# A two-block fp32 network on one core: products on disjoint tiles of the array made neighbours in TensorE's order

## The chip, the cores and the metric

The kernel runs on one core of a Trainium2 chip. The metric is the device time of one execution in microseconds (us), the median of several. TensorE (PE) multiplies; loading its stationary operand is shown as an engine of its own (PEld). VectorE (DVE), ScalarE (ACT) and GpSimd (POOL) do the rest, and SyncE (SP) issues the transfers.

## What is computed

The reference takes 256 tokens of width 1024 through two stacks of two layers each, all in fp32. Cut to what the change touches:

```python
def first_block(x, ...):           # layer 0: recurrence beside differential attention; layer 1: gated MLP
    y_r = rwkv7_mix(...)           # 8 heads of 64; in the kernel: chunks, with a triangular solve
    y_d = diff_attention(...)      # softmax(q1 k1) - lam * softmax(q2 k2), heads of 64, causal
    x = layer_norm(ALPHA * x + concat(y_r, y_d) @ w_out); x = layer_norm(ALPHA * x + conv_ffn(x))
    ...

def second_block(x, c, ctx, ...):  # 256 tokens and 256 of a context, two layers
    m = silu(c) @ w_mod + b_mod    # modulation: 1024 -> 6144, for c and for c_ctx
    h = rms_norm(x) * (1 + scale) + shift
    o_f = fourier_mix(...); o_a = window_attention(...); o_h = hgrn_bidir(...)
    x = x + gate * (sum(sigmoid(g_i) * (o_i @ w_i)) @ w_out)
    x = x + gate2 * (square(relu(h2 @ w1)) @ w2)
```

## The kernel before, in words

**Large products.** Weights stream in 512 KB tiles `wraw` (four buffers, L222), issued by SP. Each is split into a high part `whi` (ScalarE) and a low part `wlo` (VectorE), and every product is three matmuls: high by high, high by low, low by high, with 128 rows and 128 columns of the array in use.

**Small products.** Several products use only a part of the array and are in plain fp32, for which the trace has two matmuls for each call of `mm`. Five kinds of them stand in places that belong together, since they use parts that do not overlap:

- modulation (L1096, the product at L1108): for each of 8 feature chunks and 3 column quads of two layers, four products of 512 columns go to four tiles of 32 array columns, from two `wraw` tiles into one PSUM bank `sf`;
- recurrence pairs (`wkv`, L809): for each of 4 (token tile, head group) pairs and two head pairs, the products of `bt` and `kt` with `ar`, the even head on array rows 0 to 63 and the odd on rows 64 to 127, each half into a PSUM bank of its own; VectorE then multiplies each bank by a mask into `M`;
- scores, in differential attention (`scores`, L1021) and in window attention (`attention`, L1478): `qT` by `kT`, again one product on each half of the array's rows, into two banks; masks are added by further matmuls, then follow maximum, exponential, reciprocal;
- values of window attention (L1509): probabilities `PT` of two heads by `va`, one head on array columns 0 to 63, one on 64 to 127, over four key blocks (two for the context's queries and so on), into one bank;
- sums of squares (`ss_chunk`, L1200): after each fourth column chunk, the squares `sq` (four buffers for each half of the tokens, L1194) times ones, on four tiles of 32 array columns.

Banks: `ss` has two buffers (L226), `st` two, `mm` three, `sf` one. `ss` serves the recurrence, all scores and the state-space branch.

**What sets the order.** The program is written as a sequence of calls, in which generators interleave stages by hand: `fill` (L1087) puts one modulation step between steps of others, `merge` steps (L1688) go between attention steps. At build time a scheduler then sets each engine's order from the tiles' dependences and from priorities that follow the program's order. On the chip each engine takes its instructions in that order, and semaphores stand where another engine's result is needed. No product of a run is tied to the next one: what else is ready may be placed between them.

Of the kernel before, what the change touches and what calls it, by code (L numbers as in the profile page):

```python
# [18 lines left out]
S = 256  # L19
KC = D // 128  # L20
# [8 lines left out]
# columns of per-feature parameters: feature = chunk * 128 + partition  # L29
# [184 lines left out]
class Kern:  # L214
# [60 lines left out]
    def mm(self, out, lhsT, rhs, start=True, stop=True, **k):  # L275
        self.pe.matmul(out, lhsT, rhs, start=start, stop=stop, **k)  # L276
# [47 lines left out]
    def w_stat(self, out, hi, lo, xh, xl, nk, start=True, stop=True, k0=0):  # L324
        """out[cols, tok] += w^T x, weights stationary; hi, lo [128, nk * 128]."""
        for k in range(nk):
            wh, wl = hi[:, k * 128:(k + 1) * 128], lo[:, k * 128:(k + 1) * 128]
            a, b = xh[:, k0 + k], xl[:, k0 + k]
            self.mm(out, wh, a, start=start and k == 0, stop=False)
            self.mm(out, wh, b, start=False, stop=False)  # L330
            self.mm(out, wl, a, start=False, stop=stop and k == nk - 1)

    def w_stat_steps(self, out, hi, lo, xh, xl, nk):
        """w_stat in steps of two feature chunks."""
        for k in range(0, nk, 2):
            self.w_stat(out, hi[:, k * 128:], lo[:, k * 128:], xh, xl, 2, k == 0, k == nk - 2, k)
            yield

    def w_stat_k(self, items, xh, xl, nk=KC):
        """Several column chunks at once, feature chunk outermost: each chunk of x is used as it arrives.  # L340
        items: (out, hi, lo, first of its bank)."""
        for k in range(nk):
            for out, hi, lo, first in items:
                wh, wl = hi[:, k * 128:(k + 1) * 128], lo[:, k * 128:(k + 1) * 128]
                a, b = xh[:, k], xl[:, k]
                self.mm(out, wh, a, start=first and k == 0, stop=False, skip_group_check=True)
                self.mm(out, wh, b, start=False, stop=False, skip_group_check=True)
                self.mm(out, wl, a, start=False, stop=k == nk - 1, skip_group_check=True)

    def w_mov(self, outs, hi, lo, xh, xl, nk, ncol, toks, first, last, k0=0):  # L350
        """outs[i][tok, cols] += x^T w for token tile toks[i], weights moving."""
        for i, t in enumerate(toks):
            for k in range(nk):
                wh, wl = hi[:, k * ncol:(k + 1) * ncol], lo[:, k * ncol:(k + 1) * ncol]
                a, b = xh[:, k0 + k, t * 128:(t + 1) * 128], xl[:, k0 + k, t * 128:(t + 1) * 128]
                self.mm(outs[i], a, wh, start=first and i % 2 == 0 and k == 0, stop=False, skip_group_check=True)
                self.mm(outs[i], a, wl, start=False, stop=False, skip_group_check=True)
                self.mm(outs[i], b, wh, start=False, stop=last and k == nk - 1, skip_group_check=True)

    def nat_gemm(self, w, cb, xh, xl, toks, nh=2):  # L360
        """Column block cb (256 wide) of x @ w in token-major banks, two token tiles to a bank."""
        banks = [self.pmm() for _ in range(len(toks) // 2)]
        outs = [banks[i // 2][:, (i % 2) * 256:(i % 2) * 256 + 256] for i in range(len(toks))]
        for h in range(nh):
            hi, lo = self.wload(w[cb * nh + h])
            self.w_mov(outs, hi, lo, xh, xl, 4, 256, toks, h == 0, h == nh - 1, k0=4 * h)
        return [b.rearrange("p (t c) -> p t c", t=2) for b in banks]

# [42 lines left out]
    def norm_rows(self, i):  # L411
        """Gain and bias of the i-th norm, on every partition."""
        rows = self.lr.tile([128, 2, D], F32, name="lrow")
        self.nc.sync.dma_start(rows.rearrange("p a c -> p (a c)"),
                                 self.A["lnrows"][i:i + 1].partition_broadcast(128))
        return rows

    def nat_out(self, w, yh, yl, z, early=1):
        """z = ALPHA * z + y @ w; for the first column blocks the half of y that is ready first goes ahead of the other."""
# [20 lines left out]
    def last_block(self, z, yh, yl, tiles, scale=1.0, banks=None, first=True, last=True):  # L440
        """Last column block of z = scale * z + y @ w, a bank for each token tile."""
# [9 lines left out]
    def layer_norm(self, z, nm, l, rows, final=None):  # L451
        """Normalise token-major z. Gives the split transposed activations, and the norm in z, or, in the end, the
        residual of the second block."""
# [176 lines left out]
    def shift_mix(self, pool, bank, chunks, tag):  # L630
        """xs = p + mu * (previous token's p - p), features on partitions."""
# [163 lines left out]
    def wkv(self, es, side, ar, bt, kt, vn, bn, kn, gn, pend, bon, wmask, wlev, row):  # L795
# [7 lines left out]
        for t, g in groups:  # L803
            for j in (2 * g, 2 * g + 1):
                banks = [self.pss(), self.pss()]
                tk = slice(t * 128, t * 128 + 128)
                for i, w in enumerate((bt, kt)):
                    for ps, e in zip(banks, (slice(0, 64), slice(64, 128))):
                        self.mm(ps[:, i * 256:i * 256 + 256], w[e, j, tk], ar[e, j, t])  # L809
# [149 lines left out]
    def to_feat(self, y, c0, t):  # L959
        """Token-major y [128, 512] of token tile t into split chunks c0.. of the transposed activations."""  # L960
# [39 lines left out]
    def diff_attn(self, es, qT, kT, vd, row):  # L1000
# [14 lines left out]
        def scores(t, h):  # L1015
# [3 lines left out]
            for c in range(2):  # L1019
                e = slice(64 * c, 64 * c + 64)  # L1020
                self.mm(pv[c][:, :nk], qT[e, h, t * 128:(t + 1) * 128], kT[e, h, :nk], start=True, stop=False)  # L1021
# [65 lines left out]
    def fill(self, n):  # L1087
        """Emit n steps of the work that waits in self.fillers."""
# [7 lines left out]
    def modulation(self, l, quads):  # L1096
        """Columns quad * 2048.. of silu(cond) @ w_mod + b_mod, both conditions, features on partitions.
        Four 512-column blocks go through four 32-column tiles of the array."""
        for qd in quads:
            ps = self.psf()  # L1100
            for k in range(KC):
# [5 lines left out]
                for j in (2, 3, 0, 1):  # L1107
                    self.mm(ps[32 * j:32 * j + 32], self.cs[:, k],  # L1108
                            raws[j // 2][:, (j % 2) * 512:(j % 2) * 512 + 512],
                            start=k == 0, stop=k == KC - 1, skip_group_check=True)  # L1110
# [14 lines left out]
    def second_setup(self):  # L1125
        """Constants of the second block, the residual (x | ctx, features on partitions), and the context's first norm."""
# [32 lines left out]
    def lower_bounds(self, cp):  # L1159
        """Forget-gate bounds of both layers, [128, dir * 4 + head]; f = th * cf + df, k = th * ck + dk."""  # L1160
# [31 lines left out]
    def ss_chunk(self, ap, k, s):  # L1192
# [4 lines left out]
        if k % 4 == 3:  # L1197
            for k, sl, sq in [q for q in self.ssq if q[1] == sl]:
                j = k % 4
                self.mm(self.ssb[32 * j:32 * j + 32, sl], self.ones[:, 0:32], sq,  # L1200
                        start=j not in self.ss_open, stop=k >= 4, skip_group_check=True)
                self.ss_open.add(j)
            self.ssq = [q for q in self.ssq if q[1] != sl]

    def norm_half(self, ap, l, n, s):
        """Modulated norm of one half of the residual into the split hh, hl."""
# [30 lines left out]
    def head_gemm(self, banks, tiles, T, x_first=True):  # L1237
        """First products after a norm: feature chunk outermost, one half after the other."""
# [6 lines left out]
    def head_load(self, w):  # L1245
        """The first three column chunks that follow a norm, two of them into buffers of their own."""
# [4 lines left out]
    def res_chunks(self, l, m, T, w, xh, xl, gate, norm=None, head=None, out=None):  # L1251
        """X += gate * (w^T x), then the norm given by norm = (layer, index); gives the weights that head loads."""
# [145 lines left out]
    def attention(self, l, T, es, br):  # L1398
# [68 lines left out]
        for s in range(T // S):  # L1467
# [3 lines left out]
            for j in range(4):  # L1471
                PT = [ab.tile([128, 4, S], F32, name=f"PT{e}", bufs=1) for e in range(2)]
                for qt in range(2):
                    banks = [self.pss(), self.pss()]
                    for e, ps in enumerate(banks):
                        r = slice(64 * e, 64 * e + 64)
                        q = qT[r, j, s * S + qt * 128:s * S + qt * 128 + 128]
                        self.mm(ps[:, :nk], q, kT[r, k0:], start=True, stop=s == 1)  # L1478
# [26 lines left out]
                po = self.pst()  # L1505
                for k in kc:
                    for e in range(2):
                        r = slice(64 * e, 64 * e + 64)
                        self.mm(po[r, 0:S], va[:, k, r], PT[e][:, k], start=k == kc[0], stop=k == 3)  # L1509
# [33 lines left out]
    def hgrn(self, l, T, es, br, vn, side):  # L1543
# [6 lines left out]
        def parity(tl, s, o, n, B):  # L1550
            """Positions o.. of stream s: blocks of B, the even ones from tl[:, s, 0], the odd ones from tl[:, s, 1]."""
# [7 lines left out]
        def project(h, o):  # L1559
            """Gates, keys, queries and output gate of head h into o, in small steps."""  # L1560
# [127 lines left out]
    def merge(self, l, n, T, br, acc, tgp, mx=None):  # L1688
        """acc += 2 * sigmoid(gate_n) * (branch_n @ w_branch_n), in small steps; the last branch
        splits the sum into mx."""  # L1690
# [23 lines left out]
    def store(self, op, k0, n):  # L1714
        """Feature chunks k0.. of the finished residual, token-major, to the output."""
# [48 lines left out]
```

## Time and profile before

| | |
|---|---|
| median of 3 runs | 2304.64 us (2303.82 to 2312.74) |
| profiled execution, span from first to last instruction | 2304.2 us |
| TensorE busy | 2230.4 us, 97% |
| VectorE, ScalarE, GpSimd busy | 1354.0, 931.6, 294.7 us |
| transfers | 310.06 MB, 135 GB/s on average |

The profile gives no other time for the profiled execution than its span, which lies 0.4 us below the median of the runs. A group's busy time is the union of its instructions: what runs side by side is counted once, and the mean duration beside it counts each by itself. A line of the timeline gives the start, the time from the first start to the last end, and how many like instructions follow each other; an idle time in brackets comes with what ended it.

### The profile page before, as it was taken

What the parts mean: (1) busy time and instruction counts of PE and PEld (TensorE: products, weight loads), DVE (VectorE), ACT (ScalarE), POOL (GpSimd) and SP (SyncE); (2) the same over time, 40 slices, a digit from 0 to 9 for tenths busy, and PEclk for the clock granted to TensorE, in tenths of its full rate; (3) what the DMA queues carried; (4) which work ended last, traced back from release to release, by engine and by line L of the source; (5) the groups of instructions that cost most, each with busy time, mean ns of one, the idle gap of its engine ahead of it and who ended that gap; (6) DMA issues with size and microseconds to landing.
All of it is one profiled execution on the core that took longest, in us unless ns stands there. A gap on an engine that the chain in (4) does not pass through costs nothing. (4 is left out here: it accounts for less than half of the span.)

```text
span 2304.2 us, 37682 instructions
## 1 busy us (share of the span) xinstructions
PE 2230.4 (97%) x15048; PEld 1936.7 (84%) x15048; DVE 1354.0 (59%) x2361; ACT 931.6 (40%) x1589; POOL 294.7 (13%) x382
## 2 busy tenths in 40 slices
PE   8999899989999999999999999999999999999999
PEld 7867799978899988657778888888889878888999
DVE  6523777674867734665566446444345566766665
ACT  5322454442445433442333334233244443345443
POOL 1153200022100002001222000000000205420000
PEclk9999999997999999999999999999999999999999
DMA  7456666573665522123442242333333233245663
GB/s 237 135 170 212 201 206 185 171 242 95 222 188 168 174 74 83 51 85 105 150 136 74 87 119 73 92 101 92 101 111 93 74 95 94 90 133 165 183 183 128
DMA packets 90640, 310.06 MB, mean 135 GB/s; under 512 B 10257, under 2 KB 12433, under 8 KB 89826
## 3 DMA queue, kind: packets, MB, share of 16 engines
q1 hardware_dynamic: 90242, 307.30, 43.1%
q8 instruction: 118, 1.93, 0.3%
q14 instruction: 56, 0.46, 0.1%
q0 software_dynamic: 224, 0.36, 0.0%
HBM read 306.58 MB, written 1.05 MB: 134 GB/s over the span
## 5 line engine op out<-in xcount | busy, mean ns | idle before, releaser
L242 DVE TENSOR_TENSOR wlo<-wraw,whi 128x1024 fp32r<-128x1024 f32 x462 | 558.0, 1211 | 391.4 <-ACT whi L321 390.4
L321 ACT CAST whi<-wraw 128x1024 fp32r<-128x1024 f32 x494 | 492.8, 1001 | 726.2 <-PE mm L276 624.4
L276 PE MATMUL mm<-hh,whi 128*128 128x256 f32 (+1 forms) x1200 | 412.9, 346 | 4.3 <-ACT hh L254 2.4
L276 PE MATMUL mm<-hh,wlo 128*128 128x256 f32 (+1 forms) x1200 | 406.3, 339 | 0.0
L276 PE MATMUL mm<-hl,whi 128*128 128x256 f32 (+1 forms) x1200 | 405.4, 338 | 0.0
L276 PE MATMUL mm<-xh,whi 128*128 128x256 f32 x880 | 252.7, 288 | 8.2 <-ACT xh L321 7.3
L276 PE MATMUL mm<-xl,whi 128*128 128x256 f32 x880 | 253.8, 288 | 3.8 <-DVE xl L242 3.7
L276 PEld LDWEIGHTS mm<-hh,whi 128*128 128x128 f32 x1200 | 227.2, 190 | 32.4 <-issue 7.9
L276 PEld LDWEIGHTS mm<-hh,wlo 128*128 128x128 f32 x1200 | 227.7, 190 | 28.8 <-issue 3.6
L276 PE MATMUL mm<-xh,wlo 128*128 128x256 f32 x880 | 251.9, 286 | 0.0
L276 PEld LDWEIGHTS mm<-hl,whi 128*128 128x128 f32 x1200 | 228.0, 190 | 25.4 <-issue 3.1
L276 PE MATMUL mm<-whi,hh 128*128 128x256 f32 x736 | 205.9, 280 | 3.2 <-ACT vn L1326 2.4
L276 PE MATMUL mm<-whi,hl 128*128 128x256 f32 x736 | 205.6, 279 | 0.0
L276 PE MATMUL mm<-wlo,hh 128*128 128x256 f32 x736 | 205.5, 279 | 0.0
L276 PEld LDWEIGHTS mm<-xh,whi 128*128 128x128 f32 x880 | 171.5, 195 | 10.8 <-ACT xh L321 7.6
L276 PEld LDWEIGHTS mm<-xl,whi 128*128 128x128 f32 x880 | 171.8, 195 | 8.7 <-DVE xl L242 6.8
L276 PE MATMUL mm<-ul,whi 128*128 128x256 f32 (+1 forms) x536 | 176.7, 330 | 0.1
L276 PE MATMUL mm<-uh,wlo 128*128 128x256 f32 (+1 forms) x536 | 176.3, 329 | 0.0
L276 PE MATMUL mm<-uh,whi 128*128 128x256 f32 (+1 forms) x536 | 176.2, 330 | 0.0
L276 PEld LDWEIGHTS mm<-xh,wlo 128*128 128x128 f32 x880 | 171.8, 195 | 0.0
L276 PEld LDWEIGHTS mm<-whi,hh 128*128 128x128 f32 x736 | 140.0, 190 | 4.2 <-ACT vn L1326 2.8
L276 PEld LDWEIGHTS mm<-whi,hl 128*128 128x128 f32 x736 | 138.2, 188 | 0.8 <-issue 0.8
(411 smaller groups left out, 3959.8 us busy)
## 6 DMA issues: line engine op xcount, KB each, us to landing
wraw<-in_w_ff SPq DMA_DIRECT2D x128, 512.0 KB, 3.7
wraw<-in_w_mod SPq DMA_DIRECT2D x96, 512.0 KB, 4.2
wraw<-in_w_up SPq DMA_DIRECT2D x88, 512.0 KB, 3.7
wraw<-in_w_gate SPq DMA_DIRECT2D x48, 512.0 KB, 3.6
wraw<-in_w_dn SPq DMA_DIRECT2D x32, 512.0 KB, 3.6
wraw<-in_w_br SPq DMA_DIRECT2D x48, 256.0 KB, 2.6
wraw<-in_w_h SPq DMA_DIRECT2D x24, 512.0 KB, 3.7
wraw<-in_w_out SPq DMA_DIRECT2D x16, 512.0 KB, 3.8
```

Of the source, the lines that this page charges most:

```text
L242: (eng or self.dve).tensor_tensor(out, a, b, ALU.subtract)
L276: self.pe.matmul(out, lhsT, rhs, start=start, stop=stop, **k)
L321: self.act.copy(hi, src)
```

## The change

A helper `mm_run` issues a list of products. The first is issued as before. Each later one is issued with raised priority and with an edge, without synchronisation, from the one before it. `mm` now returns its instruction. The five kinds of products go through the helper, and in four of them the order within the run is turned round: the second half (or the last chunk, or `kt` before `bt`) comes first. Modulation keeps its order. The rest of the diff removes comments and docstrings.

```diff
     def mm(self, out, lhsT, rhs, start=True, stop=True, **k):
-        self.pe.matmul(out, lhsT, rhs, start=start, stop=stop, **k)
+        return self.pe.matmul(out, lhsT, rhs, start=start, stop=stop, **k)
+
+    def mm_run(self, calls):
+        first = self.mm(*calls[0][:3], **calls[0][3])
+        for out, lhsT, rhs, k in calls[1:]:
+            with self.tc.high_priority():
+                nxt = self.mm(out, lhsT, rhs, **k)
+            self.tc.add_manual_dep(
+                nxt.ins, first.ins.name,
+                mybir.DependencyInfo(mybir.DependencyClass.NoSync, mybir.DependencyReason.DATA), reason="mm_run")
+            first = nxt
...
-                for i, w in enumerate((bt, kt)):
-                    for ps, e in zip(banks, (slice(0, 64), slice(64, 128))):
-                        self.mm(ps[:, i * 256:i * 256 + 256], w[e, j, tk], ar[e, j, t])
+                halves = list(zip(banks, (slice(0, 64), slice(64, 128))))[::-1]
+                self.mm_run([(ps[:, i * 256:i * 256 + 256], w[e, j, tk], ar[e, j, t], {})
+                             for i, w in ((1, kt), (0, bt)) for ps, e in halves])
...
-            for c in range(2):
+            calls = []
+            for c in (1, 0):
                 e = slice(64 * c, 64 * c + 64)
-                self.mm(pv[c][:, :nk], qT[e, h, t * 128:(t + 1) * 128], kT[e, h, :nk], start=True, stop=False)
+                calls.append((pv[c][:, :nk], qT[e, h, t * 128:(t + 1) * 128], kT[e, h, :nk],
+                              dict(start=True, stop=False)))
+            self.mm_run(calls)
...
-                for j in (2, 3, 0, 1):
-                    self.mm(ps[32 * j:32 * j + 32], self.cs[:, k],
-                            raws[j // 2][:, (j % 2) * 512:(j % 2) * 512 + 512],
-                            start=k == 0, stop=k == KC - 1, skip_group_check=True)
+                self.mm_run([
+                    (ps[32 * j:32 * j + 32], self.cs[:, k], raws[j // 2][:, (j % 2) * 512:(j % 2) * 512 + 512],
+                     dict(start=k == 0, stop=k == KC - 1, skip_group_check=True)) for j in (2, 3, 0, 1)])
...
-                self.mm(self.ssb[32 * j:32 * j + 32, sl], self.ones[:, 0:32], sq,
-                        start=j not in self.ss_open, stop=k >= 4, skip_group_check=True)
+                calls.append((self.ssb[32 * j:32 * j + 32, sl], self.ones[:, 0:32], sq,
+                              dict(start=j not in self.ss_open, stop=k >= 4, skip_group_check=True)))
                 self.ss_open.add(j)
+            self.mm_run(calls[-1:] + calls[:-1])
...
-                    for e, ps in enumerate(banks):
+                    calls = []
+                    for e in (1, 0):
...
-                        self.mm(ps[:, :nk], q, kT[r, k0:], start=True, stop=s == 1)
+                        calls.append((banks[e][:, :nk], q, kT[r, k0:], dict(start=True, stop=s == 1)))
+                    self.mm_run(calls)
...
+                calls = []
                 for k in kc:
-                    for e in range(2):
+                    for e in (1, 0):
                         r = slice(64 * e, 64 * e + 64)
-                        self.mm(po[r, 0:S], va[:, k, r], PT[e][:, k], start=k == kc[0], stop=k == 3)
+                        calls.append((po[r, 0:S], va[:, k, r], PT[e][:, k], dict(start=k == kc[0], stop=k == 3)))
+                self.mm_run(calls)
```

## Rows read from the trace of the kernel before

**Rows 1.** The page: span, and busy time of the engines.

```profile
span 2304.2 us, 37682 instructions
PE 2230.4 (97%) x15048; PEld 1936.7 (84%) x15048; DVE 1354.0 (59%) x2361; ACT 931.6 (40%) x1589; POOL 294.7 (13%) x382
```

**Rows 2.** Who waited for whom: us in total, times, longest us.

```profile
ACT whi L321 <- PE mm L276: 624.4, 320, 4.9
```

**Rows 3.** Groups by shape: count | busy us, mean ns | idle before; fourth line: 200 to 246 us.

```profile
L276 PE MATMUL sf<-wraw,cs 128*32 128x512 f32 x384 | 68.5, 621 | 2.0 <-DMA wraw<-in_w_mod 2.0
L276 PE MATMUL ss<-kT,qT 64*128 64x512 f32 x64 | 31.1, 641 | 0.0
L276 PE MATMUL ss<-kT,qT 64*128 64x256 f32 x48 | 13.3, 428 | 0.0
L276 PE MATMUL ss<-kT,qT 64*128 64x128 f32 x16 | 3.9, 322 | 0.0
L276 PE MATMUL st<-PT,va 128*64 128x256 f32 x160 | 27.6, 390 | 0.0
L276 PE MATMUL st<-sq,ones 128*32 128x256 f32 x112 | 20.2, 391 | 0.8 <-ACT sq L254 0.8
```

**Rows 4.** Timeline of TensorE in the triangular solve: start us, us, what, count.

```profile
145.75 1.04 PE L276 MATMUL sf<-wraw,cs 128*32 128x512 f32 x2
150.28 1.04 PE L276 MATMUL sf<-wraw,cs 128*32 128x512 f32 x2
...
172.52 1.07 PE L276 MATMUL sf<-wraw,cs 128*32 128x512 f32 x8
175.94 1.06 PE L276 MATMUL sf<-wraw,cs 128*32 128x512 f32 x8
```

**Rows 5.** Timeline of TensorE at scores, of differential and of window attention.

```profile
225.76 0.70 PE L276 MATMUL ss<-kT,qT 64*128 64x256 f32 x4
915.47 1.12 PE L276 MATMUL ss<-kT,qT 64*128 64x512 f32 x2
940.26 1.63 PE L276 MATMUL ss<-kT,qT 64*128 64x512 f32 x4
949.00 1.91 PE L276 MATMUL ss<-kT,qT 64*128 64x512 f32 x4
979.51 1.13 PE L276 MATMUL ss<-kT,qT 64*128 64x512 f32 x4
```

**Rows 6.** Timeline of TensorE at the values.

```profile
944.18 1.94 PE L276 MATMUL st<-PT,va 128*64 128x256 f32 x14
1035.52 1.08 PE L276 MATMUL st<-PT,va 128*64 128x256 f32 x6
```

**Rows 7.** Timeline of TensorE at the sums of squares.

```profile
718.12 0.64 PE L276 MATMUL st<-sq,ones 128*32 128x256 f32 x8
```

**Rows 8.** Groups by shape: maximum and exponential of the scores.

```profile
L254 ACT ACTIVATE E<-ss,m 128x512 f32<-128x512 f32 x32 | 22.0, 687 | 21.8 <-DVE m L248 21.2 <-DVE m L239 0.5
L1486 DVE TENSOR_REDUCE m<-ss 128x1 f32<-128x512 f32 x32 | 21.6, 685 | 3.0 <-PE ss L276 2.7
```

**Rows 9.** Busy time in stretches: PE, PEld, DVE, ACT, POOL, clock, DMA share, GB/s.

```profile
100.00:125.00 25.00, 22.11 (x148) 16.34 (x147) 10.31 (x16) 1.76 (x3) 13.63 (x27) 1.00 0.20 66
175.00:200.00 25.00, 24.92 (x210) 18.85 (x208) 5.04 (x9) 7.86 (x15) 16.34 (x27) 1.00 0.75 253
```

**Rows 10.** Timeline of TensorE and VectorE at the pairs of the recurrence.

```profile
107.09 0.70 PE L276 MATMUL ss<-ar,bt 64*128 64x256 f32 x4
108.25 1.29 DVE L236 TENSOR_TENSOR M<-ss,wmask 128x512 f32<-128x512 f32 x2 [9.50 <-PE ss L276]
116.60 0.70 PE L276 MATMUL ss<-ar,bt 64*128 64x256 f32 x2 [0.77 <-DVE M L236]
118.51 0.70 PE L276 MATMUL ss<-ar,bt 64*128 64x256 f32 x2 [0.19 <-DVE M L236]
123.50 1.29 DVE L236 TENSOR_TENSOR M<-ss,wmask 128x512 f32<-128x512 f32 x2 [0.62 <-PE ss L276]
```

More of the change, by code (lines that the diff above doesn't have):

```diff
@@ L1505, in attention @@
                 po = self.pst()
+                calls = []
                 for k in kc:
-                    for e in range(2):
+                    for e in (1, 0):
                         r = slice(64 * e, 64 * e + 64)
-                        self.mm(po[r, 0:S], va[:, k, r], PT[e][:, k], start=k == kc[0], stop=k == 3)
+                        calls.append((po[r, 0:S], va[:, k, r], PT[e][:, k], dict(start=k == kc[0], stop=k == 3)))
+                self.mm_run(calls)
                 sl = slice(s * S, s * S + S)
```

## The prediction, made before the result was known

> **What bounds the kernel now.** I read the page first. TensorE is busy 97% of the 2304.2 us span, VectorE 59%, ScalarE 40% [rows 1]. Then I asked who waits for whom: the longest wait of the kernel is ScalarE's, 624.4 us of waiting for matmuls to give back a weight buffer before it splits the next tile [rows 2]. So the weights are ahead, TensorE is the bound nearly everywhere, and what matters is how long it is held by each product, not how late its operands are.
>
> Next, the groups of TensorE instructions by shape [rows 3]. Their busy time is a union: matmuls that run beside each other count once. An fp32 product stands in the trace as two matmuls (192 modulation products, 384 matmuls). For the five kinds that the change touches I compare this union with the length of one complete run, taken from the timeline. Modulation: eight matmuls (four products on four column tiles) take 1.07 us, but two matmuls of one product alone take 1.04 us [rows 4]. A product that stands alone therefore costs as much as four. Scores: a pair on two row tiles takes 1.13 us, one alone 1.12 us; at 256 columns a pair takes 0.70 us [rows 5]. The saving is the number of pieces into which runs are broken.
>
> That a piece really holds TensorE is seen in the triangular solve, where one kernel shows both. With one of four modulation products cut off from its run, the cycle from one such stray to the next is 150.28 - 145.75 = 4.53 us; with runs whole it is 175.94 - 172.52 = 3.42 us [rows 4]. The 1.11 us between them is one piece of 1.04 us and a little for going in and out of the column tiles. In the whole-run stretch the DMA engines were 75% busy at 253 GB/s [rows 9], and TensorE 24.92 of 25 us: the faster pace was fed.
>
> **The change part by part.** *The helper.* Returning the instruction, the order edge (without synchronisation) and the priority add no instruction: TensorE should keep 15048 matmuls [rows 1]. Cost nothing on chip; if some edges became semaphore waits, it would show as time in which the engine waits for nothing visible, a rival below.
>
> *Modulation, L1108.* 48 runs of four. Now 68.5 us; whole 48 x 1.07 = 51.4; gain 17.1 us [rows 3, 4]. The order of the products does not change, so their transfers are waited for as before. Buffers of `wraw` come free earlier, which lets SP issue the next load earlier.
>
> *Scores, L1021 and L1478.* Each fp32 call gives two matmuls: 64, 48 and 16 matmuls are 16, 12 and 4 pairs. At 512 columns 31.1 - 16 x 1.13 = 13.0 us; at 256, 13.3 - 12 x 0.70 = 4.9; at 128, I let the 3.9 us halve, 1.9, as if none of the four pairs were whole now; the other end is 0, if all were [rows 3, 5]. Sum 19.8 us. The upper half now goes first, so a run waits until both `ss` banks are free, where half of it could go when the first was. Queued behind it on TensorE is whatever was placed next; waiting for it are the maximum (0.685 us) and the exponential (0.687 us) of each half [rows 8]. Cover: a bank pair's round is 1.1 us for the run and 2.1 for two maxima and one exponential; with as much as the run again for masks and gaps, an estimate, some 4.3 us. Runs of scores stand 8.7 us apart (940.26 to 949.00) [rows 5, 8], so there are 4 us of slack with merge products between. If that cover goes, the whole 19.8 is at stake.
>
> *Values, L1509.* 12 runs: eight of eight products (four key blocks, two heads; four in each layer) and four of four (the context's queries, first layer). The first product goes alone now, when the first half's probabilities are there, and the rest follows later, as 14 or 6 matmuls [rows 6]. 8 x 1.95 + 4 x 1.08 = 19.9 against 27.6: gain 7.7 us; 1.95 is the 14 matmuls at 1.94, to which two more go beside others. The run starts with the half that VectorE copies last.
>
> *Sums of squares, L1200.* 56 products are 14 runs: 20.2 - 14 x 0.64 = 11.2 us [rows 3, 7]. Three squares of a run are held until the fourth is there. They have four buffers; the next square is one column chunk later and the run itself is 0.64 us, so this costs nothing; without that gap it would be up to 0.64 us for ScalarE, 14 times.
>
> *Pairs of the recurrence, L809.* Here the cover is missing. In the steady part a unit takes 118.51 - 116.60 = 1.91 us because one bank is filled while VectorE reads the other, and TensorE waits on M [rows 10]. With the upper half first, a run starts after both reads: 1.16 us from a whole run's start to the first read (107.09 to 108.25), and 1.29 for two reads: 2.45 us. Eight units end at 107.09 + 8 x 2.45 = 126.7 instead of 123.50 + 1.29 = 124.8: **1.9 us lost**. The other end: of the 1.91 us TensorE is idle 0.19 and held 1.72, where a whole run holds it 1.16; if modulation runs move into the gap, 8 x 0.56 = 4.5 us are won [rows 10]. I take the loss, since the stretch shows TensorE idle for M already.
>
> The Trainium skill (TensorEngine Tiling (Array Packing), section PSUM Bottleneck) says that tiling speeds up TensorE and not the emptying of PSUM, which may then bound. Rows 10 agree for the recurrence; elsewhere the slack above speaks against it. By it the scores' part would be left out of the sum, which is the first rival.
>
> *Sum.* 17.1 + 19.8 + 7.7 + 11.2 = 55.8 us of TensorE time. Not all becomes time: the emptiest of the stretches with such runs shows TensorE busy 22.11 of 25 us (88%), another 24.92 [rows 9]. As work leaves, stretches come nearer to the first; I take 88%: 49.3. Less 1.9: 47.4 us. The profiled execution has a span of 2304.2 us, 0.4 below the median of the runs, 2304.64; I count from the median: **2257 us**. With 100% and the 4.5 us it would be 2304.6 - 60.3 = 2244.
>
> **Rivals.** *Bank hand-over takes the scores' gain.* Runs wait for the second bank, and 19.8 us come back as waits on ScalarE's exponential. For: two banks only, and the recurrence shows it. Against: the 4 us of slack. (55.8 - 19.8) x 0.88 - 1.9 = 29.8: 2275 us. The rule quoted above from the Trainium skill (TensorEngine Tiling (Array Packing), PSUM Bottleneck) would end here.
>
> *Half is lost to new waits.* The order on TensorE is fixed ahead, and moving a hundred runs shifts what stands between; chains now hidden (transposes of E, of Q) come out. For: TensorE sits idle for 2.9 of 25 us where its operands come out of short chains [rows 9]. Against: the stretch with the whole modulation runs stayed full. 27.9 - 1.9 = 26.0: 2279 us.
>
> *It does not do what it says.* If the scheduler lets other ready work between a product and its follower, runs stay as they are: 2304.6 us, no change.
>
> *Slower: the head of the queue.* A run begins with the operand that comes last, and TensorE issues in order, so if that operand is later on the chip than where the run was placed, everything behind waits. The place is the start of the 48 + 32 + 12 + 14 + 8 = 114 runs; the price is bounded by the worst adjacent pair now, 1.91 us where 1.13 would do [rows 5], 0.78 us. At that price everywhere 89 us against 55.8: 2338 us. It decides from 0.49 us a run on. Against: other pairs waited far less (1.63 us, a 0.50 us wait, and none at 979.51).
>
> **How the numbers follow.** Forecast 0.64, bank hand-over 0.13, half lost 0.11, no effect 0.06, slower 0.06. The range reaches from just below all gains with none lost (2242) past the two rivals of the same sign (2283) and leaves out the last two. About 0.5% (11.5 us) is what a measurement can tell from no change: forecast and the first two rivals are faster by more, 0.88; 0.06 same; 0.06 slower.
>
> **What would show it.** Right: modulation's busy time near 51 us in 48 stretches of eight matmuls; scores near 18, 8 and 2; values near 20; squares near 9; a solve cycle of 3.4 us throughout; the recurrence's pairs about 2.45 us apart. Wrong: the same unions as now (no effect); unions fallen, but TensorE's idle time up, before scores on ScalarE (hand-over) or before transposes and weights elsewhere (half lost); waits at the head of runs near 0.5 us each (slower).

## The result, and the profile of the changed kernel

The changed kernel takes **2280.2 us** (median of 4 runs, 2275.4 to 2283.8) where the kernel before took 2304.3 in the same series: a ratio of **0.9885 [0.9865, 0.9905]**, some 24 to 27 us less. The forecast was 2257, the range 2242 to 2283. The direction was right, and the time lies in the range, but only about half of the forecast gain came. The profiled execution took 2280.6 us with a span of 2278.7.

The page of the changed kernel, its span and the busy time of the engines, answers to [rows 1]:

```profile
span 2278.7 us, 37674 instructions
PE 2192.4 (96%) x15048; PEld 1933.4 (85%) x15048; DVE 1352.7 (59%) x2361; ACT 930.6 (41%) x1589; POOL 293.6 (13%) x382
```

The number of matmuls is the same, and TensorE is held 38.0 us less (2230.4 - 2192.4). The span fell by 25.5 us, so 12.5 us of the work that went became idle time. The groups by shape of the changed kernel (count, busy us and mean ns of one, idle time before) answer to [rows 3]:

```profile
L276 PE MATMUL sf<-wraw,cs 128*32 128x512 f32 x384 | 52.7, 623 | 7.9 <-DMA wraw<-in_w_mod 7.8
L276 PE MATMUL ss<-kT,qT 64*128 64x512 f32 x64 | 24.7, 641 | 0.2 <-ACT E L254 0.2
L276 PE MATMUL st<-PT,va 128*64 128x256 f32 x160 | 19.9, 386 | 0.1
L276 PE MATMUL ss<-kT,qT 64*128 64x256 f32 x48 | 12.2, 452 | 2.6 <-ACT E L254 2.6
L276 PE MATMUL st<-sq,ones 128*32 128x256 f32 x112 | 8.5, 389 | 1.4 <-ACT sq L254 1.4
L276 PE MATMUL ss<-kT,qT 64*128 64x128 f32 x16 | 2.9, 322 | 0.0
```

Modulation, values and squares came out as forecast (51.4, 19.9, 9.0). The scores of 512 columns did not (24.7 for 18.1). And one number is new: modulation now waits 7.8 us for its weights, where it waited 2.0 before [rows 3].

**Where the time went.** I cut both traces at the same five instructions: the first pair of the recurrence, the first `N,T` product of the triangular solve, its last `Q,Z` product, the first product on the next `xh`, which ends the differential attention, the output projection and a norm, and the last product of the kernel. The table holds the stretches between them in each profiled execution (kernels of the experiments below included), in us.

| kernel | pairs | solve | attention to next xh | all after |
|---|---|---|---|---|
| before | 17.2 | 75.0 | 85.6 | 2015.4 |
| the change | 27.4 | 68.7 | 87.2 | 1983.3 |
| no_pairs | 17.2 | 70.6 | 83.9 | 1982.7 |
| only_pairs | 35.1 | 73.9 | 83.9 | 2014.5 |
| hold_mod | 27.4 | 69.0 | 93.9 | 1978.8 |
| only_mod | 17.2 | 68.9 | 91.9 | 2009.3 |
| pairs_banks | 11.0 | 70.5 | 83.9 | 1986.8 |
| no_pairs_banks | 10.8 | 70.3 | 83.6 | 1979.9 |

After the first `xh` product the change gains 32.1 us; in the three stretches ahead of it, taken together, it gives back 5.5 (183.3 for 177.8). The pairs' stretch alone is 10.1 us longer, where 1.9 were forecast. Its timeline on TensorE (start us, us, what, count, idle time before and what ended it) answers to [rows 10]:

```profile
113.90 0.70 PE L276 MATMUL ss<-ar,kt 64*128 64x256 f32 x2 [0.78 <-DVE M L236]
115.45 1.07 PE L276 MATMUL sf<-wraw,cs 128*32 128x512 f32 x8 [0.85 <-DMA wraw<-in_w_mod]
116.44 0.48 PE L276 MATMUL ss<-ar,kt 64*128 64x256 f32 x1
...
123.27 1.07 PE L276 MATMUL sf<-wraw,cs 128*32 128x512 f32 x8 [1.49 <-DMA wraw<-in_w_mod]
...
127.15 0.70 PE L276 MATMUL ss<-ar,kt 64*128 64x256 f32 x4
129.23 1.06 PE L276 MATMUL sf<-wraw,cs 128*32 128x512 f32 x8 [0.94 <-DMA wraw<-in_w_mod]
130.22 0.70 PE L276 MATMUL ss<-ar,kt 64*128 64x256 f32 x4
135.67 1.14 PE L276 MATMUL ss<-T,N 128*128 128x128 f32 x8
```

Eight modulation runs now stand in this stretch, where there were 1.75 (counted in the trace). They were drawn into the holes that a pair leaves while it waits for two banks, they wait there for weights, and the pairs queue behind them: the unit at 127.15 is followed at 130.22, 3.07 us later. At 113.90 a run is even torn (so are those at 110.36 and 118.35): one product goes, the modulation run comes between, the other product follows.

Later these runs are missing. In the differential attention, where three fewer stand than before (5 for 8), the waits of TensorE between 105 and 262 us show a long one, and the busy time in three windows (PE, PEld, DVE, ACT, POOL, granted clock, DMA share, GB/s) shows a low clock:

```profile
PE sf L276 <- DMA wraw<-in_w_mod: 4.4, 5, 1.5
PE ss L276 <- ACT E L254: 2.6, 1, 2.6
```

```profile
218.00:230.00 12.00, 11.70 (x153) 8.89 (x149) 8.04 (x27) 8.27 (x21) 0.00 (x0) 1.00 0.30 100
230.00:243.70 13.70, 10.58 (x42) 8.69 (x42) 7.75 (x19) 4.60 (x18) 3.35 (x4) 0.50 0.31 107
231.00:246.00 15.00, 11.88 (x78) 9.78 (x76) 7.44 (x19) 4.53 (x17) 3.35 (x4) 0.58 0.23 75
```

The granted clock is 0.58 from 231 to 246 us, so most of that window ran at the lower level of 1.2 GHz, and a score product of 256 columns took 1.22 us instead of 0.70. In the kernel before it was 1.00 throughout. The long wait did not bring this about: the clock was down from 230 us on, after 12 us in which TensorE was busy for 11.70, and the wait of 2.6 us ended only at 236.02:

```profile
236.02 1.22 PE L276 MATMUL ss<-kT,qT 64*128 64x256 f32 x2 [2.63 <-ACT E L254]
```

### The profile page after: what moved, and what is told of

Read it like the earlier page. It is cut to its first block, busy times and chain, and to the rows that moved or that the text cites. A ratio compares the mean times of both kernels' runs of the same rounds, so it can differ in the third digit from the quotient of the medians.

```text
span 2278.7 us, 37674 instructions
## 1 busy us (share of the span) xinstructions
PE 2192.4 (96%) x15048; PEld 1933.4 (85%) x15048; DVE 1352.7 (59%) x2361; ACT 930.6 (41%) x1589; POOL 293.6 (13%) x382
```

## The experiments

Before them, three theories. **A**: the pairs leave holes, modulation is drawn in, waits, and is missing later, where the clock falls for want of it. **B**: only the hand-over of both banks costs. **C**: the priority of the modulation runs draws them forward by itself. Each ratio below is to the kernel before in the same series.

**The pairs undone, and the pairs alone.** no_pairs is the change with L809 as before; only_pairs is the kernel before with the helper and this edit alone:

```
-                halves = list(zip(banks, (slice(0, 64), slice(64, 128))))[::-1]
-                self.mm_run([(ps[:, i * 256:i * 256 + 256], w[e, j, tk], ar[e, j, t], {})
-                             for i, w in ((1, kt), (0, bt)) for ps, e in halves])
+                for i, w in enumerate((bt, kt)):
+                    for ps, e in zip(banks, (slice(0, 64), slice(64, 128))):
+                        self.mm(ps[:, i * 256:i * 256 + 256], w[e, j, tk], ar[e, j, t])
```

> The change with only the recurrence's pairs as they were before (bt ahead of kt, no run, lower half first). Theory A (the paired products of the recurrence leave holes on TensorE, modulation runs are drawn into them, wait there for their weights and are missing as filler in the differential attention at 225 to 262 us): the stretch to the first N,T product ends near 125 us instead of 135.7, a modulation run stands between transposes and merge products at 225 to 262 us, the granted clock at 231 to 246 us is back at 1.00, and the time falls by 15 to 23 us to 2257 to 2265. Theory B (only the hand-over of both banks costs, 1.9 us as forecast): 2277 to 2279. Theory C (the priority of the modulation runs draws them forward whatever the pairs do): the stretch is as in the change, 2275 to 2284.

> The kernel before with only the recurrence's pairs made runs (kt ahead of bt, upper half first). Theory A: slower than before by 5 to 15 us (2309 to 2320), with modulation products in the pairs' stretch that wait for weights, and a granted clock well below 1 somewhere at 225 to 262 us. Theory B: 2306 to 2307, pairs 2.45 us apart. Theory C: no modulation products more than before in the pairs' stretch, 2303 to 2307.

Measured: no_pairs 0.9835 [0.9814, 0.9856], median 2268.9; only_pairs **1.0067 [1.005, 1.0085]**, median 2321.7. Undoing one of five edits takes the gain from 1.15% to 1.65%; that edit alone makes the kernel slower by about 15 us. Both medians lie a little beyond A's ranges. B's 1.9 us falls, and C too: without the pairs two modulation runs stand in the stretch, not eight. The stretch is 17.2 us with the pairs undone and 35.1 with them alone. Why alone it is worse than in the change is in the timeline of only_pairs, where the modulation products are still loose:

```profile
113.65 0.70 PE L276 MATMUL ss<-ar,kt 64*128 64x256 f32 x2
117.00 1.93 PE L276 MATMUL sf<-wraw,cs 128*32 128x512 f32 x6 [2.65 <-DMA wraw<-in_w_mod]
118.86 0.79 PE L276 MATMUL ss<-ar,kt 64*128 64x256 f32 x1
...
121.17 1.05 PE L276 MATMUL sf<-wraw,cs 128*32 128x512 f32 x2
```

Here a modulation run is six matmuls and two, in two places, and holds TensorE twice. One part of A's expectation failed: no low clock at 225 to 262 us in only_pairs (1.00), though only six modulation runs stand in its attention stretch and eight before.

**The modulation runs held behind the pairs.** If A is the whole story, this mends the change (`run` is the first product of a modulation run, `last_pair` that of the last recurrence run):

```
-                self.mm_run([(ps[:, i * 256:i * 256 + 256], w[e, j, tk], ar[e, j, t], {})
+                self.last_pair = self.mm_run([(ps[:, i * 256:i * 256 + 256], w[e, j, tk], ar[e, j, t], {})
...
+                if getattr(self, "last_pair", None) is not None:
+                    self.tc.add_manual_dep(
+                        run.ins, self.last_pair.ins.name,
+                        mybir.DependencyInfo(mybir.DependencyClass.NoSync, mybir.DependencyReason.DATA), reason="hold")
```

> The change, with one order edge more: each modulation run that is emitted after the recurrence's pairs may not stand ahead of the last of the last unit's pairs on TensorE (an order edge without synchronisation). Theory A: the pairs come about 2.45 us apart and the first N,T product at about 128 us, the modulation runs of that stretch stand at 225 to 262 us again, and the time falls to 2260 to 2268. Theory B (the pairs' own hand-over is the cost, and the modulation runs only fill its idle time): the first N,T product still comes at 133 us or later, and 2275 to 2284.

Measured: 0.989 [0.9873, 0.9907], median 2280.9, the same as the change. A as stated falls: the stretch is 27.4 us again, now with two modulation runs instead of eight. B's case came (the first `N,T` product at 135.3 us, and 2280.9), though not at B's price. The timeline and the busy time in stretches of hold_mod say why:

```profile
109.83 1.08 PE L276 MATMUL ss<-ar,kt 64*128 64x256 f32 x3 [0.79 <-DVE M L236]
112.34 1.12 PE L276 MATMUL ss<-ar,kt 64*128 64x256 f32 x3 [0.78 <-DVE M L236]
...
119.24 1.39 PE L276 MATMUL ss<-ar,kt 64*128 64x256 f32 x3 [0.79 <-DVE M L236]
```

```profile
107.90:113.00 5.10, 3.52 (x21) 2.02 (x20) 2.58 (x4) 0.58 (x1) 2.33 (x6) 1.00 0.00 0
113.00:135.00 22.00, 19.51 (x75) 10.83 (x74) 7.04 (x11) 1.76 (x3) 10.86 (x20) 0.53 0.05 10
```

At full clock the units come 112.34 - 109.83 = 2.51 us apart: the prediction's 2.45 was right. But TensorE stood idle for 0.8 us of each, and from 113 us on its granted clock is 0.53, nearly all of it the lower of its two levels. In the change, with fillers in the holes, the clock stays at 1.00 and the fillers cost the time; here, almost without them, the low clock costs it. The Trainium skill (TensorE: Matmul & The Clock Gate, section on the HAM clock gate) says that the lower clock is the state of rest, which activity lifts. These rows agree in part: the clock fell after a window in which TensorE was busy for 3.52 of 5.10 us, but it stayed down while TensorE was busy for 19.51 of 22.

That the hole makes the clock fall is likely, not shown. no_pairs and no_pairs_no_diff (an experiment below) have the same products in the same order in this stretch, with much the same holes that the kernel before has there; the clock stayed up in the profiled execution of one and fell in that of the other, which took 2.5 us more:

```profile
107.10:124.30 17.20, 14.34 (x85) 8.69 (x85) 9.84 (x16) 1.17 (x2) 13.05 (x26) 1.00 0.34 123
107.60:127.30 19.70, 17.47 (x86) 10.84 (x85) 9.90 (x15) 1.17 (x2) 13.28 (x26) 0.80 0.31 107
```

**The hole taken away.** What makes the run wait is that both banks of the last unit must have been read. So the units take banks in turn from two pools; pairs_banks keeps the runs, no_pairs_banks has the products as before:

```
-                banks = [self.pss(), self.pss()]
+                banks = [self.pss(), self.pss()] if j % 2 == 0 else [self.pmm(), self.pmm()]
```

> The change, with the recurrence's units taking their two banks in turn from the ss pool and from the mm pool, so that a run need not wait for the reads of the unit just before. If the hand-over of both banks is what costs in the pairs' stretch: no modulation run between the units, units 1.3 us apart (the two reads of VectorE, 0.645 us each) instead of 2.5 to 4.2, the first N,T product within 13 to 18 us of the first pair instead of 27.4, and 2262 to 2270. If the reads or GpSimd's Q set the stretch whatever the banks: still over 22 us to the first N,T product, and 2275 to 2284. A halved clock (TensorE idle while GpSimd makes Q) would show as a granted clock below 0.8 there.

> The same banks in turn, but with the recurrence's products in the order of before and without runs, the other runs as in the change. If it is the run that gains once the banks are there: the stretch to the first N,T product is 1 to 4 us longer than with runs. If the banks alone do it: the same stretch within 0.5 us, and the same time as with runs within 3 us (2262 to 2270).

Measured: pairs_banks **0.9832 [0.981, 0.9853]**, median 2264.3; no_pairs_banks 0.9824 [0.9805, 0.9842], median 2263.1. The stretch falls from 27.4 to 11.0 us with runs and from 17.2 to 10.8 without. So the hand-over of banks was the cause, and with banks enough the runs gain nothing at all here: VectorE sets the pace. The whole time does not tell either kernel from no_pairs (0.9835 [0.9814, 0.9856]), in which the pairs are merely as before. In no_pairs_banks its reads of M follow each other without a gap, and in the stretch it is busy 9.65 of 10.90 us at a granted clock of 1.00:

```profile
108.85 1.29 DVE L236 TENSOR_TENSOR M<-ss,wmask 128x512 f32<-128x512 f32 x2 [9.50 <-PE ss L276]
110.05 1.28 DVE L236 TENSOR_TENSOR M<-mm,wmask 128x512 f32<-128x512 f32 x2
111.25 1.28 DVE L236 TENSOR_TENSOR M<-ss,wmask 128x512 f32<-128x512 f32 x2
```

```profile
107.60:118.50 10.90, 10.90 (x79) 7.29 (x77) 9.65 (x16) 1.17 (x2) 8.74 (x18) 1.00 0.00 1
```

The Trainium skill (TensorEngine Tiling (Array Packing), Gotcha 1: PSUM Pressure) says that row tiles which work side by side write to different banks, so that tiling asks for more of them. The case agrees, with 27.4 against 11.0 us.

**The other edits, each alone on the kernel before** (the edits are those of the change, so no diff):

> The kernel before with only the modulation products made runs. Theory A (the pairs of the recurrence draw modulation forward, not modulation itself): all 48 runs whole, busy time 52 to 54 us, the solve's cycle 3.4 us from its start, no more modulation runs in the pairs' stretch than before, and a gain of 13 to 17 us (2287 to 2291). Theory C: modulation runs are crowded into the pairs' stretch and wait for weights there, and the gain is under 8 us (2297 to 2305).

> The kernel before with only the values and the sums of squares made runs. By the forecast 7.7 + 11.2 = 18.9 us of TensorE time, 88% of it 16.6 us: 2288. Theory F (these stages are TensorE-bound, so what the runs save is all gained): 16 to 19 us (2286 to 2289). Theory G (new waits at the head of the runs take half): 7 to 11 us (2294 to 2298).

> The kernel before with only the score pairs made runs (differential attention and second block). By the forecast: 19.8 us of TensorE time, 88% of it in the time, 17.4 us, so 2287 from 2304.6. Theory D (the first product of a run is given whichever bank is freed first, and its follower waits in the middle of the run for the second bank, so only part of the runs are whole): the union of the score products falls by 6 to 9 us only and the gain is 3 to 9 us (2296 to 2302). Theory E (hand-over: the runs are whole and wait at their head on ScalarE's exponential for as much as they save): union down by about 16 us, idle time before the scores up by as much, 2302 to 2308.

Measured: only_mod 0.9947 [0.9928, 0.9966], about 12 us; only_vs 0.9918 [0.9899, 0.9937], about 19 us; only_scores 0.9983 [0.9966, 1.0001], about 4 us and not clear of no change. Values and squares give all that they save (theory F). Modulation gives a little under the bound of A, all 48 runs whole (51.6 us), and the solve 6 us shorter as forecast; C falls again. In the profiled execution of only_mod the attention stretch is 6.3 us longer than before, and one row says why:

```profile
231.00:246.00 15.00, 15.00 (x99) 12.11 (x100) 5.13 (x12) 5.77 (x14) 0.00 (x0) 0.50 0.20 64
```

The waits ahead of it are of 0.6 us at most, and yet the clock is at its lower level for all of it. The seven timed executions of this one kernel lie between 2291.2 and 2304.1 us, with mean clocks from 0.989 to 0.981, so it does not fall equally in every execution. Only_scores spreads the same way (2298.2 to 2317.5). Scores alone save little, as D said: 28.7 us for 512 columns, 31.1 before.

**Why the score runs are not whole.** In the change, six of the sixteen pairs of 512 columns take 1.13 us as a whole run does; eight take 1.21 to 1.99 us, and two 3.1 us with other work between. Three rows of the change show why:

```profile
945.86 0.69 ACT L254 ACTIVATE E<-ss,m 128x512 f32<-128x512 f32 x1 [0.44 <-DVE m L1511]
946.08 1.73 PE L276 MATMUL ss<-kT,qT 64*128 64x512 f32 x4
946.69 0.29 PEld L276 LDWEIGHTS ss<-kT,qT 64*128 64x128 f32 x2 [0.31 <-ACT E L254]
```

The first product of the run starts while the exponential still reads the second bank of the run before, and the other product waits for that bank in the middle of the run. Which half takes which bank the trace does not name. whole_scores adds an edge to no_pairs, so that a run stands behind the exponential that frees the second bank; no_pairs_no_diff takes the runs out of the differential attention:

```
+                    if getattr(self, "last_exp", None) is not None:
+                        self.tc.add_manual_dep(
+                            run.ins, self.last_exp.ins.name,
+                            mybir.DependencyInfo(mybir.DependencyClass.NoSync, mybir.DependencyReason.DATA), reason="hold")
```

> The change without the recurrence's runs, and with one order edge more: in the second block a score run may not stand ahead of the exponential that frees the second bank of the unit before it. Theory D: all or nearly all of the second block's runs are whole (1.13 us at 512 columns, 0.70 at 256), nothing new waits, and the time is 3 to 7 us below the kernel without that edge (2262 to 2266 if that one is at 2268.9). Theory E: the wait in the middle of the run becomes a wait at its head, no gain (2267 to 2271).

> The change without the recurrence's runs and without the runs of the differential attention's scores. If those runs hold up the chain of the differential attention (wait for E's bank, 2.63 us at 236 us in the change): the stretch from the end of the solve to the first block's output projection falls from 83.9 by 2 us or more, and the time to 2262 to 2266. If they only save what their wholeness saves (under 2 us): 2269 to 2271, the stretch 0 to 2 us longer.

Measured: whole_scores 0.987 [0.9845, 0.9896], median 2277.2, no gain over no_pairs. Its profiled execution is slower than that of no_pairs only in the first block, which the edit does not touch and where the clock fell (19.7 us in the pairs' stretch, 89.7 in the attention stretch; after it 1982.2, in no_pairs 1982.7). no_pairs_no_diff 0.9841 [0.9816, 0.9866], median 2268.9, is the same as no_pairs, so the runs of the differential attention neither help nor harm measurably. The miss in whole_scores is read in its timeline: the order is as wanted, but an edge without synchronisation sets only the place, and TensorE comes to that place before the exponential is done:

```profile
946.69 0.69 ACT L1512 ACTIVATE E<-ss,m 128x512 f32<-128x512 f32 x1 [0.28 <-DVE m L239]
946.91 1.74 PE L276 MATMUL ss<-kT,qT 64*128 64x512 f32 x4
```

The exponential frees its bank at 947.38; the run starts at 946.91 with one half and is held for 1.74 us instead of 1.13.

**Filler for the differential attention.** If it is want of work that lets the clock fall there, four modulation steps moved from the solve should keep it up (no_pairs with the first line once and the second at four places):

```
-                self.fill(1)
+                self.fill(0 if lev > 1 and (t, g) == (1, 1) else 1)
...
-        self.fill(1)
+        self.fill(2)
```

> The change without the recurrence's runs, and with four of the modulation steps moved from the solve (one of four after its first level) to the four places in the differential attention where one step stands, so that two stand there. If idle time of TensorE lets its clock fall in the differential attention and a filler prevents it: the granted clock is 1.00 from 225 to 265 us in the profile and the times of the runs lie within 6 us of each other (2262 to 2270). If it is no matter of filler: as the kernel without the move, 2264 to 2275, or slower by what the weights are waited for there.

Measured: 0.9868 [0.9847, 0.9889], median 2276.1: no faster than no_pairs, rather slower (the intervals overlap), and a miss. With ten modulation runs instead of seven in the stretch the clock fell all the same:

```profile
231.00:246.00 15.00, 15.00 (x108) 10.03 (x107) 3.67 (x12) 1.98 (x6) 0.00 (x0) 0.50 0.15 48
```

So what lets the clock fall in the differential attention stays open. The number of fillers does not decide it, nor does the order of the products: no_pairs, pairs_banks, no_pairs_banks, hold_mod and whole_scores have the same products in the same order in the attention stretch, seven modulation runs among them, and it took 83.6 to 83.9 us in the first three, where the clock stayed up, and 93.9 and 89.7 in the last two, where it fell. In a profiled execution where it falls it costs some 6 to 12 us: 99.5 us here, 3.2 of them for three more runs of 1.07 us.

**Banks for the scores too.** The same remedy as for the pairs, on top of no_pairs_banks, for every second score run of the second block:

```
-                    banks = [self.pss(), self.pss()]
+                    banks = [self.pss(), self.pss()] if qt == 0 else [self.pmm(), self.pmm()]
```

> The kernel with the recurrence's banks in turn and its products as before, and in the second block the score runs of the second query tile in banks of the mm pool. If the second bank's hand-over is what breaks the score runs: nearly all runs of 512 columns are whole at 1.13 us, the union of the score products falls from about 37 to 30 to 33 us, and the time is 3 to 7 us below the kernel without that edit (2256 to 2260 if that one is at 2263). If the mm banks are missed more by the merge products than the scores gain: the union falls but the time does not (2261 to 2270), with idle time of TensorE before merge products. If the hand-over is not the cause: the same union within 1 us and 2261 to 2266.

Measured: **0.9795 [0.9781, 0.981]**, median 2261.1, the lowest ratio of the study. Its interval lies below those of the change and of no_pairs, and overlaps that of no_pairs_banks. Its groups by shape for 512 columns, and three runs of the first layer's scores in its timeline:

```profile
L276 PE MATMUL ss<-kT,qT 64*128 64x512 f32 x32 | 10.1, 641 | 0.0
L276 PE MATMUL mm<-kT,qT 64*128 64x512 f32 x32 | 10.1, 641 | 0.1
```

```profile
938.29 1.13 PE L276 MATMUL mm<-kT,qT 64*128 64x512 f32 x4
943.34 1.13 PE L276 MATMUL ss<-kT,qT 64*128 64x512 f32 x4
952.11 1.13 PE L276 MATMUL mm<-kT,qT 64*128 64x512 f32 x4
```

The second bank was what broke the runs: 14 of 16 are whole now, 20.2 us where no_pairs_banks has 24.8. Whether that reaches the time is less clear: the profiled spans of the two kernels are 2255.8 and 2256.1 us, though the edit took 4.6 us off these products. TensorE idles 4.5 us more after the first `xh` product, and 3.0 us of waiting are new before merge products, which share those banks, as the second case had expected (this row stands in score_banks alone of the two):

```profile
PE mm L276 <- DVE acc L251: 3.0, 3, 1.4
```

## Why the prediction was half right

*Modulation, values, squares.* The unions were forecast as 51.4, 19.9 and 9.0 us and are 52.7, 19.9 and 8.5. Reading the price of a stray from one kernel's own whole and broken runs [rows 4, 6, 7] works. The three together were forecast at 0.88 x 36.0 = 31.7 us; alone they gave about 12 + 19 = 31. That the sum agrees is luck. The 88% was no common factor: values and squares gave all, modulation about 0.7.

*"The order of the products does not change, so their transfers are waited for as before."* This is the first step that failed. The order inside a run stayed; the place of the run among other work did not. Six runs stood earlier, and 7.8 us of waiting for weights took the place of 2.0, 4.4 of it in the pairs' stretch.

*Pairs of the recurrence, "1.9 us lost".* This term was mis-sized: alone it is about 15 us. Its mechanism, a run that waits for two reads, was right, and so was 2.45 us per unit (2.51). What the step left out is what TensorE does in the 0.8 us that come up idle in a unit. The other end of the bound assumed that modulation in that gap was a gain of 4.5 us; the runs showed that it waits there for its weights, and that where it was kept out, in hold_mod, the clock fell.

*Scores, 19.8 us.* The second mis-sized term: in the change the union fell by 8.5 us, alone the time by about 4. The step that failed is "a run waits until both `ss` banks are free". It does not: it starts on the first, and is held in the middle by the second. The 4 us of slack were mis-sized too. They set a round of 4.3 us, an estimate, against one distance of 8.7 us; the next one before was 5.7 (949.00 to 954.68). In the change the run at 939.73 has its second bank read by 945.86 + 0.69 = 946.55, a round of 6.8 us, and the next run starts at 946.08. The rival of the bank hand-over had the right place and more than half of the price: 11.3 of the 19.8 us did not come.

*The sum.* With what the edits gave alone, 12 + 19 + 4 - 15 = 20 us, against 24 to 27 measured, each term being uncertain by some 4 us. The rival "half is lost to new waits" gave 2279 and was right in size and partly in kind: there were new waits, for weights and for banks. But of the 12.5 us of new idle time only 2.8 lie in the pairs' stretch, 5.1 in the attention stretch, 1.4 in the solve and 3.1 after it; the pairs' 10.1 us are mostly TensorE busy with modulation ahead of them. The rival "slower" asked for 0.49 us lost in each of 114 runs; eight pairs alone were that bad, and only_pairs shows what it looks like.

## What to carry over

A run of products that go side by side is whole only when all its output banks are free: before making one, count the banks that its stage turns over, and add banks first. With banks enough, the stage here fell from 27.4 to 11.0 us, and the run itself was worth nothing. A change that moves the places of work is forecast by asking what will be drawn into each new hole and what that work waits for, and what its old place does without it.

## Not expected of the hardware

TensorE's granted clock fell to its lower level (0.53 over 22 us in hold_mod) in a stretch where it was idle for no more than 0.8 us at a time, and stayed at 1.00 in the same stretch of the change, with modulation runs in the gaps. In the differential attention it read 0.50 over 15 us in only_mod after waits of 0.6 us at most, and in the change it fell after 12 us in which TensorE was busy for 11.70. It is no property of the kernel alone: with the same products in the same order it fell in one profiled execution and not in another, which made 17.2 or 19.7 us of the pairs' stretch and 83.9 or 93.9 of the attention stretch. What sets it off is not shown here. A forecast that counts busy time alone misses it, and a stretch is to be compared between two kernels only with the granted clock beside it.
